# Two more gates computed by seven products, and a sigmoid moved, in a hybrid attention block

## The chip, the cores and the metric

The kernel runs on one core of one Trainium2 chip. The metric is device time in microseconds for one execution of the whole program; smaller is better. The time before is 1466.01 us, the median of three runs (1466.0 to 1467.67 us).

Five engines work side by side, each executing its own instructions in order: TensorE (PE, matrix products; its weight loads are listed as PEld), VectorE (DVE), ScalarE (ACT), GpSimd (POOL) and SyncE (SP), which issues the transfers between device memory and the core.

## The reference, cut to what matters

One layer over 1024 tokens of width 1024, in float32. A single input projection gives queries, keys and values for two branches of 8 heads each (64 columns a head) and two gates of 1024 columns each:

```
proj = x @ w_in                        # 1024 x 5120: 2 x (q, k, v of 512), 2 gates of 1024
yA = softmax attention over a band of 9 chunks of 64, with a bias by distance
yB = stick-breaking attention, strictly causal, in blocks of 128 queries
mix = sigmoid(gA + bA) * (yA @ w_proj_a) + sigmoid(gB + bB) * (yB @ w_proj_b)
x = LN(alpha * x + mix @ w_out)
x = LN(alpha * x + ffn(x))             # SwiGLU
```

In the kernel the gates are cut into 16 tiles of 128 channels by 1024 tokens, numbered 0 to 15. Tile 2c is channel group c of gate A, tile 2c + 1 the same group of gate B; "pair" c is both.

## The kernel before, in words

Every matrix product is made of three (high x high, high x low, low x high parts of its operands), so that it reaches float32 precision. One such matmul has a 128x128 weight and 512 columns.

The program is written as one list of steps in Python. A scheduler makes of it one instruction stream per engine when the kernel is built, and moves loads and other work ahead where their inputs allow it. Within an engine the stream is then fixed. Tiles live in pools with few buffers (`SLOTS`): 8 of kind `op` for loaded weights and reloaded data, 3 of kind `gt` for gates, 4 of kind `kp`. A load can be issued only when the buffer's last reader is done. All loads and stores go through SP in order.

- **Stage 1 (0 to 348 us), the input projection.** It runs over pairs of 128-column pieces of `w_in`. For a pair, `prep_left`, `prep_right` and `prep_last` (L128 to L157) load two weight tiles and build sums of them; `pair_steps` (L174) then does seven products instead of eight half products, each of 12 matmuls (`product`, L159 to L172), and DVE and ACT combine the results. Queries, keys, values and the first five gate pairs are made so: `work` (L221 to L229) lists them, `project` (L325) writes the results, and `out_g` (L363) stores a raw gate tile to device memory (`g_dr`). The bias of the gates, `bg`, is loaded after the third pair (L285).
- **Branch A (about 348 to 472 us), eight heads a0 to a7.** Each head has 12 value steps. ACT takes exponentials (L507), DVE maxima and reciprocals (L501, L511), POOL the scaling (L512), PE transposes (L570) and the products with the values (L583, L584); `pv` has one PSUM bank, which a copy on ACT or DVE (L591, L598) empties.
- **Branch B (about 472 to 675 us), eight heads b0 to b7.** The same value steps, with sigmoids (L539, L540), scans (L542) and a multiplication on POOL (L547).
- **Fillers.** Between the steps of the heads, matmuls of other work are put: a generator `fill_all` (L611) yields them one by one, and `FILL` (L39) says how many a head gets in branches A and B. They are, in order: the remaining gates, one at a time (`gate`, L414: 48 matmuls each, with a weight load, cast and subtraction by `load_w`, L397), and then the projection of branch A's output. For that, `reload_y` (L651) loads a tile of the attention's output, casts it on ACT (L656) and subtracts on POOL (L657); `reload_gate` (L659) loads a gate tile and takes its sigmoid on ACT; 24 matmuls per channel group (L630) and a multiplication on DVE (L633) follow. What is not done when the last head ends runs behind it.
- **Behind branch B (675 to 722 us)** the same is done for branch B's output (L747 to L764), with `reload_gate` for gate B. Then come the output projection, the layer norms and the FFN, in the same way as before and after the change.

The first branch's order is set by `vsteps` (L706 to L733): at each step a goal rises by `FILL[branch] / 12`, and fillers are emitted until their number reaches it:

```
goal += FILL[hd["br"]] / nhead
fill_until(0.5 * (last + goal))
...
fill_until(goal)
```

Of the kernel before, what the change touches and what calls it, by code (L numbers as in the profile page):

```python
# [13 lines left out]
AF = mybir.ActivationFunctionType  # L14
# [21 lines left out]
LAG = 2  # L36
LEAD = ((6, 7, 9, 9, 10, 10, 11, 11, 12, 12, 13, 13), (7, 8, 9, 9, 10, 10, 11, 11, 12, 12, 13, 14))

FILL = (18.0, 42.0)  # L39

# [5 lines left out]
def hybrid_trunk_kernel(ctx: ExitStack, tc, x, xt, w_in, b_gate, rel_bias, w_proj,  # L48
# [6 lines left out]
    nc = tc.nc  # L55
# [12 lines left out]
    def cycle(tags, name, dtype=F32):  # L68

        turn_of[tags] = turn_of.get(tags, -1) + 1  # L70
        return slot(tags[turn_of[tags] % len(tags)], name, dtype)
# [3 lines left out]
    def bank(tag, name):  # L75
        return ps.tile([P, HW], F32, tag=tag, name=name, bufs=BANKS[tag])
# [13 lines left out]
    bg = cst.tile([P, 16], F32, name="bg")  # L90
# [17 lines left out]
    def split(dst_h, dst_l, src):  # L108
        nc.scalar.copy(dst_h, src)  # L109
        nc.vector.tensor_tensor(dst_l, src, dst_h.bitcast(F32), ALU.subtract)  # L110
# [63 lines left out]
    def pair_steps(nm, W, ops, c, done, xtag="mm"):  # L174


        st = {}

        def begin(key, tag, p):
            st[key] = bank(tag, f"{key}{nm}")  # L180
            product(st[key], W, ops, p, True)

        def add(dst, src):
            nc.vector.tensor_tensor(dst, src, dst, ALU.add)  # L184

        def p1():
            begin("sx", xtag, 1)
            nc.scalar.copy(c("11"), st["sx"])

        def p2():  # L190
            begin("sy", "sc", 2)
            add(c("11"), st["sy"])
            done("11", None)

        def p6():
            product(st["sx"], W, ops, 6, False)
            nc.scalar.copy(c("12"), st["sx"])

        def p5():
            begin("sz", "sc", 5)  # L200
            nc.scalar.copy(c("22"), st["sz"])

        def p7():
            product(st["sx"], W, ops, 7, False)
            add(c("22"), st["sx"])
            done("22", None)

        def p3():
            product(st["sz"], W, ops, 3, False)
            add(c("12"), st["sz"])  # L210
            done("12", None)

        def p4():
            product(st["sx"], W, ops, 4, False)
            done("21", st["sx"])

        return [p1, p2, p6, p5, p7, p3, p4]
# [7 lines left out]
            if i % 2:  # L225
                work.append(("v", br * 4 + i - 1, br * 12 + 8 + i - 1, br * 12 + 8 + i))

    N_GATE = 5
    work += [("g", j, 24 + j, 32 + j) for j in range(N_GATE)]  # L229
    Wa = [dict() for _ in work]  # L230

# [3 lines left out]
    def right(i):  # L235
        prep_right(Wa[i], f"p{i}", w_in[work[i][3]], "op")
        prep_last(Wa[i], f"p{i}", "kp")
# [47 lines left out]
    def small_inputs():  # L285

        rel_sb = cycle(QKV, "rel_sb")[0:8, 0:896]
        rel_in = cycle(QKV, "rel_in")[0:8, 0:N_REL]
        dma(rel_in, rel_bias)
        nc.vector.tensor_copy(rel_sb[:, 383:896], rel_in[:, ::-1])  # L290
        nc.vector.tensor_copy(rel_sb[:, 0:383], rel_in[:, 512:513].to_broadcast([8, 383]))
        dma(rel_dr, rel_sb)
        dma(bg, b_gate)

    def store_hl(d, hi, lo):
        for h in range(2):
            rows = slice(h * DH, (h + 1) * DH)
            dma(d[h * P:h * P + DH], hi[rows].bitcast(F32))
            dma(d[h * P + DH:(h + 1) * P], lo[rows])
# [25 lines left out]
    def project(i):  # L325
        kind, pair = work[i][:2]
        tl = {}

        def tile_of(side):
            if side not in tl:  # L330
                tl[side] = cycle(QKV, f"c{side}_{i}")
            return tl[side]

        def c(name):
            return tile_of(name[1])[:, (LO, HI)[int(name[0]) - 1]]

        def out_qk(side):
            scale = (-0.125 if pair < 4 else 0.125) if side == "1" else 1.0
            t = tl[side]
            h = cycle(QKV, f"hi{side}_{i}", F32R)  # L340
            nc.scalar.activation(h, t, AF.Copy, scale=scale)
            nc.vector.scalar_tensor_tensor(t, t, scale, h.bitcast(F32), ALU.mult, ALU.subtract)
            d = (q_dr, k_dr)[side == "2"]
            store_hl(d[pair], h, t)

        def out_v(side):
            pr = pair + int(side) - 1
            vs = [cycle(QKV, f"v{pr}_{h}", F32R).rearrange("p (t c) -> p t c", t=8)
                  for h in range(2)]
            for hf in range(2):  # L350
                tp = bank("tr", f"vtp{pr}_{hf}")
                for j in range(4):
                    o = hf * HW + j * P
                    tr(tp[:, j * P:(j + 1) * P], tl[side][:, o:o + P], ident)
                t3 = tp.rearrange("p (t c) -> p t c", t=4)
                ts_ = slice(4 * hf, 4 * hf + 4)
                for h in range(2):
                    split(vs[h][:, ts_, 0:DH], vs[h][:, ts_, DH:P],
                          t3[:, :, h * DH:(h + 1) * DH])
            for h in range(2):  # L360
                dma(v_dr[2 * pr + h].rearrange("p (t c) -> p t c", t=8), vs[h].bitcast(F32))

        def out_g(side):  # L363
            dma(g_dr[2 * pair + int(side) - 1], tl[side])

        out = dict(qk=out_qk, v=out_v, g=out_g)[kind]

        def done(name, acc):
            if name == "21":
                nc.scalar.copy(c("21"), acc)  # L370
                out("1")
            elif name == "12":
                out("2")

        return pair_steps(f"p{i}", Wa[i], ops_x, c, done)
# [35 lines left out]
    def load_gate(i, lo_eng):  # L411
        return load_w(w_in[24 + (i % 2) * 8 + i // 2], f"g{i}", of("op"), of("op"), lo_eng)

    def gate(i, w):  # L414
        gt = slot("gt", f"gate{i}")
        for hf, cs in enumerate((LO, HI)):
            acc = bank("mm", f"gps{i}_{hf}")
            for k in range(KT):
# [13 lines left out]
              lambda i: right(i + 1), lambda i: small_inputs() if i == 2 else None)  # L432
    first_gate = 2 * N_GATE
    first_w = load_gate(first_gate, nc.vector)
# [176 lines left out]
    def fill_all():  # L611
        w = first_w
        for i in range(first_gate, 16):
            nxt = load_gate(i + 1, nc.gpsimd) if i < 15 else load_proj(0, 0, "op", nc.gpsimd)
            yield from gate(i, w)
            w = nxt
        for i in range(4):
            reload_y(i, nc.gpsimd)
        for cc in range(4):
            nxt = load_proj(0, cc + 1, "op", nc.gpsimd) if cc < 3 else None  # L620
            for j in range(2):
                c = 2 * cc + j
                t = slot("gt", f"gA{c}")
                reload_gate(t, c, 0)
                for hf, cs in enumerate((LO, HI)):
                    acc = bank("mm", f"yAps{c}_{hf}")
                    for k in range(4):
                        ks = slice(j * HW + k * P, j * HW + (k + 1) * P)
                        for n, (lw, rx) in enumerate(((w[0], yh), (w[0], yl), (w[1], yh))):
                            mm(acc, lw[:, ks], rx[k][:, cs], start=(k == n == 0),  # L630
                               stop=(k == 3 and n == 2))
                            yield 1.0
                    nc.vector.tensor_tensor(t[:, cs], acc, t[:, cs], ALU.mult)  # L633
                if c < KEEP:
                    dma(m_dr[c], t)
                else:
                    kept[c] = t
            if cc < 3:
                reload_y(4 + cc, nc.gpsimd)
            w = nxt  # L640
# [18 lines left out]
    def reload_gate(t, c, br):  # L659
        dma(t, g_dr[2 * c + br])  # L660
        col = br * 8 + c
        nc.scalar.activation(t, t, AF.Sigmoid, bias=bg[:, col:col + 1])

    fill = fill_all()
    state = dict(t=0.0, done=False)
# [1 line left out]
    def fill_until(t):  # L667
        while state["t"] < t and not state["done"]:
            try:
                state["t"] += next(fill)  # L670
            except StopIteration:
                state["done"] = True
# [36 lines left out]
    for si, (hd, g, st, box) in enumerate(vsteps):  # L709
# [17 lines left out]
        last = goal  # L727
        goal += FILL[hd["br"]] / nhead
        fill_until(0.5 * (last + goal))
# [395 lines left out]
```

## Time and profile before

| | |
|---|---|
| median of three runs | 1466.01 us |
| the profiled execution | 1465.81 us |
| its span, first to last instruction | 1464.0 us |
| mean granted TensorE clock | 0.995 of full speed |
| PE busy | 1432.2 us |
| DVE, ACT, POOL busy | 1025.3, 679.4, 278.1 us |
| instructions on PE, DVE, ACT, POOL | 6740, 1637, 1179, 326 |

A row of the timeline gives the start, the duration, the engine, the line of the kernel, the operation, and output<-input by the names of the tiles; in brackets stands how long the engine was idle just before, and what it waited for. A row of the chain gives the start, the duration and the work that the end of the program depended on at that time. The page's slices cut the span in 40 parts and give the busy share of each in tenths. A row of a tile's view gives line, engine, operation and count, then the shortest, median and longest duration in nanoseconds.

### The profile page before, as it was taken

To read this page: it belongs to the slowest core of one execution; us is meant where nothing else is said; L and a number is where in the kernel's file an instruction comes from. 1 tells how busy PE (TensorE), PEld (TensorE's weight loads), DVE (VectorE), ACT (ScalarE), POOL (GpSimd) and SP (SyncE) were. 2 spreads that over 40 slices of the span, in tenths; PEclk is the share of its full clock that TensorE was granted. 3 is DMA by queue.
4 is the path that set the end of the run, shared out by engine and by line. 5 is a ranking of instruction groups with operands and counts; after the bars stand their busy time and mean duration, and the time that the engine had idled before them with its cause. 6 is when DMAs were issued, how large, how long until landed. Compare 5 with 4: busy or idle time off the path is not lost.

```text
span 1464.0 us, 19115 instructions
## 1 busy us (share of the span) xinstructions
PE 1432.2 (98%) x6740; PEld 1184.4 (81%) x6740; DVE 1025.3 (70%) x1637; ACT 679.4 (46%) x1179; POOL 278.1 (19%) x326
## 2 busy tenths in 40 slices
PE   8999999999999998999999999999999999999997
PEld 6788888887888787878888888888888888888886
DVE  8856655434776876887848966777776665978767
ACT  6444444335878878775413534444444433221201
POOL 0000000003555879760004100000000000100016
PEclk9999999999999999999999999999999999999999
DMA  6565545338666476856611123444444457887602
GB/s 216 158 188 173 157 145 177 124 99 249 188 196 206 131 217 184 238 179 247 232 43 72 50 95 130 158 154 148 152 151 145 152 195 247 301 308 235 213 15 101
DMA packets 83455, 247.72 MB, mean 169 GB/s; under 512 B 10512, under 2 KB 10512, under 8 KB 83360
## 3 DMA queue, kind: packets, MB, share of 16 engines
q1 hardware_dynamic: 83360, 246.51, 51.5%
q8 instruction: 53, 0.87, 0.3%
q14 instruction: 42, 0.34, 0.1%
HBM read 162.03 MB, written 80.77 MB: 166 GB/s over the span
## 4 chain that ended last, share of the span: by engine, by line
PE 86%; DVE 5%; DMA 3%; ACT 3%; issue 2%; POOL 1%; SPq 0%; POOLq 0%; DVEq 0%; ACTq 0%
PE sxf L171 16%; PE sxp L171 12%; PE szf L171 8%; PE dx L1058 6%; PE szp L171 6%; PE syf L171 4%; PE gps L421 3%; PE dz L1058 3%; PE syp L171 3%; PE yAps L630 2%; PE ops L117 2%; PE ops L119 2%; PE ops L116 2%; PE fpswh_h L119 1%; PE fpswh_h L116 1%
## 5 line engine op out<-in xcount | busy, mean ns | idle before, releaser
L1014 POOL TENSOR_TENSOR wdyt<-wdyt 128x512 f32<-128x512 f32 x8 | 10.8, 1352 | 513.6 <-DMA wdgt<-in_w_ffn_out_dram 429.1
L547 POOL TENSOR_TENSOR w_b<-w_b,kp_b 128x511 f32<-128x511 f32 (+3 forms) x96 | 96.2, 1010 | 39.0 <-DVE kp_b L542 27.0
L542 DVE TENSOR_TENSOR_SCAN kp_b<-kp_b,ident_ps 128x512 f32<-128x512 f32 (+2 forms) x64 | 56.4, 883 | 24.8 <-ACT kp_b L539 24.3
L482 POOL MEMSET bias<- 64x64 f32 x8 | 1.2, 144 | 329.7 <-ACT bias L481 329.7
L778 POOL TENSOR_TENSOR mv<-mv,neghalf 128x1 f32<-128x1 f32 x16 | 23.8, 1489 | 210.3 <-DVE mv L777 210.3
L184 DVE TENSOR_TENSOR c<-sxp,c 128x512 f32<-128x512 f32 x16 | 11.1, 691 | 74.2 <-issue 41.1
L539 ACT ACTIVATE kp_b<-sc_b 128x512 f32<-128x512 f32 (+3 forms) x96 | 50.0, 521 | 24.9 <-PE sc_b L465 23.2
L110 DVE TENSOR_TENSOR pt_b<-tp_b,pt_b 128x512 fp32r<-128x512 f32 (+1 forms) x96 | 50.4, 543 | 13.8 <-ACT pt_b L109 13.5
L989 DVE TENSOR_TENSOR x<-dx,x 128x512 f32<-128x512 f32 x64 | 43.5, 686 | 17.0 <-PE dx L1058 16.9
L171 PE MATMUL szf<-x1S63h,wcf 128*128 128x512 f32 x168 | 55.1, 389 | 0.0
L109 ACT CAST pt_b<-tp_b 128x512 fp32r<-128x512 f32 (+1 forms) x96 | 48.2, 515 | 7.7 <-PE tp_b L570 6.1
L110 DVE TENSOR_TENSOR sl<-h,sl 128x512 fp32r<-128x512 f32 x56 | 38.4, 685 | 18.8 <-ACT sl L109 18.8
L512 POOL TENSOR_SCALAR w_a<-w_a,st_a 128x640 f32<-128x640 f32 (+2 forms) x64 | 42.6, 670 | 45.1 <-DVE st_a L511 33.5
L109 ACT CAST sl<-h 128x512 fp32r<-128x512 f32 x56 | 34.7, 619 | 34.5 <-PE syf L171 17.1
L110 DVE TENSOR_TENSOR pt_a<-tp_a,pt_a 128x512 fp32r<-128x512 f32 (+1 forms) x96 | 45.8, 486 | 6.8 <-ACT pt_a L109 5.5
L540 ACT ACTIVATE w_b<-sc_b 128x511 f32<-128x511 f32 (+3 forms) x96 | 50.2, 523 | 0.0
L570 PE MATMUL tp_b<-ident,w_b 128*128 128x128 f32 x288 | 48.7, 279 | 1.5 <-DVE pt_b L110 1.1
L116 PE MATMUL ops<-wh_o,mh 128*128 128x512 f32 x128 | 50.2, 392 | 0.0
L119 PE MATMUL ops<-wh_o,ml 128*128 128x512 f32 x128 | 50.0, 391 | 0.0
L117 PE MATMUL ops<-wl_o,mh 128*128 128x512 f32 x128 | 49.9, 390 | 0.0
L109 ACT CAST pt_a<-tp_a 128x512 fp32r<-128x512 f32 (+1 forms) x96 | 39.7, 426 | 19.2 <-PE tp_a L570 17.8
L507 ACT ACTIVATE w_a<-w_a,st_a 128x640 f32<-128x640 f32 (+2 forms) x64 | 44.7, 698 | 6.4 <-DVE st_a L501 5.9
(1883 smaller groups left out, 4811.4 us busy)
## 6 DMA issues: line engine op xcount, KB each, us to landing
s_dr<-sl SPq DMA_DIRECT2D x112, 256.0 KB, 2.1
sd<-s_dr SPq DMA_DIRECT2D x56, 512.0 KB, 4.5
wLf<-in_w_ffn_in_dram SPq DMA_DIRECT2D x22, 512.0 KB, 4.3
wRf<-in_w_ffn_in_dram SPq DMA_DIRECT2D x22, 512.0 KB, 3.6
wLp<-in_w_in_dram SPq DMA_DIRECT2D x17, 512.0 KB, 5.4
wRp<-in_w_in_dram SPq DMA_DIRECT2D x17, 512.0 KB, 4.2
v_dr<-v SPq DMA_DIRECT2D x16, 512.0 KB, 4.6
qs<-q_dr SPq DMA_DIRECT2D x16, 512.0 KB, 5.3
```

Of the source, the lines that this page charges most:

```text
L109: nc.scalar.copy(dst_h, src)
L110: nc.vector.tensor_tensor(dst_l, src, dst_h.bitcast(F32), ALU.subtract)
L116: mm(acc, lh, rh, start=(i == 0), stop=False)
L117: mm(acc, lh, rl, start=False, stop=False)
L119: mm(acc, ll, rh, start=False, stop=(i == n))
L171: mm(acc, lw[:, ks], rx, start=(first and kt == i == 0), stop=(kt == 3 and i == 2), skip_group_check=not first)
L539: nc.scalar.activation(kp[:, c0:e], sc[:, 0:n], AF.Sigmoid, scale=-1.0)
L540: nc.scalar.activation(be[:, m0:e], sc[:, m0 - c0:n], AF.Sigmoid)
L542: nc.vector.tensor_tensor_scan(kp[:, 0:e], kp[:, 0:e], ident_ps()[:, 0:e], 0.0, ALU.mult, ALU.add)
L547: nc.gpsimd.tensor_tensor(be[:, m0:e], be[:, m0:e], kp[:, m0 - 1:e - 1], ALU.mult)
L570: tr(tp[:, (qb - lo_q) * P:(qb - lo_q + 1) * P], wt[qb - q0][:, (kb - qb) * P:(kb - qb + 1) * P], ident)
L1058: mm(acc, a, b, start=(first and i == n == 0), stop=(i == n - 1 == 1), skip_group_check=not first)
```

## The change

The number of gate pairs that stage 1 computes by seven products rises from five to six: gates 10 and 11 leave the fillers, so that 12 of 16 gates are made in stage 1 and four (12 to 15) as fillers. For the 12, the sigmoid with its bias is taken in `out_g`, in place, before the store; `reload_gate` then takes it only for channel groups 6 and 7. `FILL` goes from 18 and 42 to 8 and 40 matmuls a head. The number of fillers falls from 480 (288 for gates, 192 for the projection) to 384 (192 and 192), and 8 x 8 + 8 x 40 = 384.

```
-FILL = (18.0, 42.0)
+FILL = (8.0, 40.0)
...
-    N_GATE = 5
+    N_GATE = 6
     work += [("g", j, 24 + j, 32 + j) for j in range(N_GATE)]
...
         def out_g(side):
+            col = (int(side) - 1) * 8 + pair
+            nc.scalar.activation(tl[side], tl[side], AF.Sigmoid, bias=bg[:, col:col + 1])
             dma(g_dr[2 * pair + int(side) - 1], tl[side])
...
     def reload_gate(t, c, br):
         dma(t, g_dr[2 * c + br])
         col = br * 8 + c
-        nc.scalar.activation(t, t, AF.Sigmoid, bias=bg[:, col:col + 1])
+        if c >= N_GATE:
+            nc.scalar.activation(t, t, AF.Sigmoid, bias=bg[:, col:col + 1])
```

From `out_g` on, the lines of the changed kernel have numbers higher by two (L507 before is L509 after), and by three behind `reload_gate`.

## The prediction

> **What bounds the kernel now.** I read the totals and the slices of the page first, then windows by stage, then PE's waits and the chain of work around the longest of them, and last ACT's timeline at the borders of the stages.
>
> ```profile
> PE 1432.2 (98%) x6740; PEld 1184.4 (81%) x6740; DVE 1025.3 (70%) x1637; ACT 679.4 (46%) x1179; POOL 278.1 (19%) x326
> PE   8999999999999998999999999999999999999997
> PE 86%; DVE 5%; DMA 3%; ACT 3%; issue 2%; POOL 1%; SPq 0%; POOLq 0%; DVEq 0%; ACTq 0%
> ```
>
> TensorE is the bound: busy 98% of the span, and 86% of the chain that ended last. A change pays through fewer or cheaper matmuls, or through the little idle time that PE has. The windows show where that is (columns: window, its length, then busy us and count for PE, PEld, DVE, ACT, POOL; granted clock; DMA share; GB/s).
>
> ```profile
> 271.66:290.70 19.04, 19.04 (x85) 15.77 (x84) 8.85 (x11) 6.03 (x9) 0.00 (x0) 1.00 0.33 111
> 348.00:472.00 124.00, 119.69 (x724) 102.41 (x724) 93.44 (x344) 98.10 (x244) 67.37 (x92) 1.00 0.70 196
> 472.00:675.00 203.00, 193.53 (x1050) 160.59 (x1049) 154.83 (x223) 160.36 (x351) 145.76 (x185) 0.97 0.63 190
> ```
>
> The first row is one whole gate pair of stage 1, from its first product to that of the next pair: PE has no gap, the other engines work less than half the time. Branch A (second row) has 4.31 us of PE idle time, branch B (third) 9.47 us, and there the clock is 0.97.
>
> **The change, part by part.**
>
> *Stage 1: one pair more, +19.04 us.* Pair 5 (gates 10 and 11) takes seven products of 12 matmuls, 84 in all; by the first row above that is 19.04 us, 0.2267 us a matmul. Its DVE work (8.85) and ACT work (6.03) lie beside PE. Its two weight loads replace the two that the gates had as fillers, and its two stores replace theirs.
>
> *The two gates leave the fillers, -21.77 us ideally.* They were 2 x 48 = 96 matmuls of the same 128x512 shape: 96 x 0.2267 = 21.77. So the saving in matmuls alone is 12 x 0.2267 = 2.72 us; the rest of the forecast is about waits. In the built instruction order of the two kernels, branch A (with what runs ahead of its first head) has 158 fillers before and 75 after; branch B has 322 and 309. That is 83 x 0.2267 = 18.82 in A and 13 x 0.2267 = 2.95 in B. The 83 are spread unevenly: ahead of the first head 14 become 21; head a0 8 becomes 5; a1 to a6, with 18 each, become 2, 2, 4, 8, 8, 8; a7 28 becomes 17. A's ACT and POOL also lose the work of the gates (casts, copies, subtractions); the bound below is a row of a head that had little of it.
>
> *What A loses by having fewer fillers, +3.5 us (0 to +8.2).* Fillers are what PE does while a head waits for its softmax.
>
> ```profile
> 357.01:373.06 16.05, 14.32 (x90) 12.13 (x88) 12.61 (x48) 11.94 (x34) 5.79 (x10) 1.00 0.77 176
> 373.06:389.63 16.57, 16.26 (x100) 13.99 (x99) 12.82 (x49) 14.15 (x38) 9.99 (x16) 1.00 0.63 175
> 439.34:455.90 16.56, 16.11 (x103) 14.10 (x102) 12.35 (x44) 12.80 (x32) 9.80 (x12) 1.00 0.70 212
> 360.09 0.53 PE L465 MATMUL sc_a<-kl,qs 128*128 128x320 f32 x2 [0.98 <-DMA kl<-k_dr]
> 372.43 0.41 PE L464 MATMUL sc_a<-kh,qs 128*128 128x320 f32 x1 [0.52 <-DVE st_a L501]
> ```
>
> The three windows are heads a0 (8 fillers), a1 and a5 (18 each). With 18 fillers PE is idle 0.31 and 0.45 us a head; with 8 it is idle 1.73, of which 0.98 is the wait for a load of keys (fourth row), so 0.75 by itself, 0.52 of that in one wait for DVE's row maximum (last row). The slope is (0.75 - 0.31) / 10 = 0.044 us a filler. So a1 and a2 would be idle 1.01 and a3 0.93, where a head of 18 has 0.31: +2.0 together; a4 to a6 0.44 more each: +1.3; a0 +0.13. That is +3.5. Heads of two fillers would then need 16.57 - 16 x 0.2267 + 0.70 = 13.6 us, for which DVE has 12.6 and ACT under 12.8 us of work: tight, so the lower end (PE stays as busy as now, 0) is not the likely one. The upper end is that no head gets shorter than a0 without its load, 16.05 - 0.98 = 15.07. Then a1 to a6 save 6 x 1.50 = 9.0 and not the 76 x 0.2267 = 17.2 that their fillers held: +8.2. I take 3.5, the slope of the neighbouring rows.
>
> *Start of A, +0.5 us (0 to +2.4).* The sigmoid of gate 11 now follows the last DVE sum of pair 5, and ACT must then change its table to the exponential.
>
> ```profile
> 348.51 1.05 ACT L404 CAST wh_g<-wr_g 128x1024 fp32r<-128x1024 f32 x1
> 349.67 0.83 ACT L507 ACTIVATE w_a<-w_a,st_a 128x640 f32<-128x640 f32 x1
> L662 ACT ACTIVATE gA<-gA,bg x8: 1151/1154/1463, 565.1 to 645.4; 128x1024 f32<-128x1024 f32 x8
> 469.18 1.28 ACT L539 ACT_TABLE_LOAD   x1
> 470.47 0.60 ACT L539 ACTIVATE kp_b<-sc_b 128x512 f32<-128x512 f32 x1
> 471.09 1.28 ACT L507 ACT_TABLE_LOAD   x1
> 472.90 1.28 ACT L540 ACT_TABLE_LOAD   x1
> ```
>
> In the built order sigmoid and table load stand between this cast and the first exponential: 1.15 + 1.28 = 2.43 us later. On SP the loads of head a1's keys and queries are queued behind the gate stores, which now wait for the sigmoids. Seven more fillers, 1.59 us, lie ahead of the first head. 2.43 - 1.59 = 0.84 would remain if nothing else covers it, and 2.43 if PE runs the fillers too soon; I take 0.5. The row at 470.47 begins 0.01 us after the load ends, so a table costs 1.28 on ACT here. The Trainium skill ("ScalarE: Activation LUTs", section "What ACT_TABLE_LOAD costs") says a switch is 1.28 us and a drain of 1.38 behind it, 2.66 in all; the trace shows no such drain, and by the page this term would be up to 1.4 higher.
>
> *The other sigmoids and tables, 0.* The ten others in stage 1 take 1.15 us each, 2.3 a pair, where ACT has 13 of 19 us free; one of them brings a table load (1.28). They leave branch B and the stage behind it. At the border of A and B (rows above) three table loads become one. That is 2.56 us less of ACT, but PE has fillers there (42 a head), so I count nothing, down to -1.3.
>
> *Stall 1 in branch B, -5.0 us (-6.5 to 0).* The longest wait of the stage comes from the reload of the attention's output for branch A's projection (chain of work first, then the timeline):
>
> ```profile
> 565.80 2.38 POOL yl L657
> 568.19 6.98 DMA yraw<-y_dr
> 576.52 0.60 ACT yv_b L598
> 568.04 1.46 ACT L662 ACTIVATE gA<-gA,bg 128x1024 f32<-128x1024 f32 x1
> 575.20 1.04 ACT L656 CAST yh<-yraw 128x1024 fp32r<-128x1024 f32 x1 [3.91 <-DMA yraw<-y_dr]
> 577.16 0.80 PE L583 MATMUL pv_b<-pt_b,v 128*128 128x512 f32 x1 [3.50 <-ACT yv_b L598]
> 560.00:580.00 20.00, 16.09 (x78) 12.53 (x77) 12.59 (x18) 15.42 (x31) 20.00 (x22) 0.91 0.84 224
> 577.16:584.20 7.04, 7.04 (x24) 6.13 (x25) 4.40 (x8) 5.47 (x11) 6.96 (x6) 0.58 0.18 58
> ```
>
> The load of the fifth y tile waits for a buffer until POOL's subtraction ends, takes 6.98 us to land, and ACT, which executes in order, stands 3.91 us at its cast (L656) with the copy that PE needs (L598) queued behind. PE loses 3.50, and then 7.04 x (1 - 0.58) = 2.96 to the clock: 6.5 in all. In the built order of the changed kernel the first four reloads and their subtractions stand earlier against attention, since the gates end 13 fillers sooner; the fifth load is issued behind the store of gate 15, and 19 ACT instructions stand between that gate's last copy and the cast. At 15.42 / 31 = 0.50 us each that is 9.5 us, against 7 for the load and some 2 for four SP issues ahead of it. So the load lands about in time. POOL has no slack there (20.00 of 20.00), and the next weight, two ACT instructions later, lands behind it: I leave 1.5 us of wait. Without the earlier order 6.5 would stay. What is late next is that weight's cast.
>
> *The two smaller stalls, -0.5 and +0.5 us.*
>
> ```profile
> 601.60 1.15 ACT L662 ACTIVATE gA<-gA,bg 128x1024 f32<-128x1024 f32 x1 [1.39 <-DMA gA<-g_dr]
> 603.65 0.50 PE L583 MATMUL pv_b<-pt_b,v 128*128 128x512 f32 x1 [1.04 <-ACT yt L598]
> 648.24 1.09 ACT L656 CAST yh<-yraw 128x1024 fp32r<-128x1024 f32 x1
> 650.20 1.05 ACT L404 CAST wh_y<-wr_y 128x1024 fp32r<-128x1024 f32 x1 [0.49 <-DMA wr_y<-in_w_proj_dram]
> 653.87 0.50 PE L583 MATMUL pv_b<-pt_b,v 128*128 128x512 f32 x1 [1.94 <-DVE yt L591]
> 653.87:658.37 4.50, 4.50 (x19) 4.00 (x19) 4.29 (x8) 2.48 (x6) 2.79 (x3) 0.62 0.30 84
> ```
>
> At 601.60 ACT waits for a gate's load before a sigmoid that the change takes away; half of PE's 1.04 us, as the multiplication (L633) still needs the load: -0.5 (-1.04 to 0). At 653.87 PE waits 1.94 us and loses 4.50 x 0.38 = 1.71 to the clock. The last reload (L656) now stands five ACT instructions earlier and may wait longer for its data, while the sigmoid at 645 stays: +0.5 (-3.65, the stall gone, to +3.65, one such stall more).
>
> On the clock, the row at 577.16 stands behind 3.50 us of idle PE and the row at 653.87 behind 1.94, both at about 0.6; behind 1.04 us at 603.65 no drop follows. So a wait of about 2 us counts nearly double. The Trainium skill ("TensorE: Matmul & The Clock Gate", "What's actually happening") ties the slow state to an idle window of about 3.4 us. The first stall agrees, the second (1.94 us) does not. By the page what I leave of stall 1 would not touch the clock; by the trace, at 2 us, it would add up to 1.7.
>
> *The sum.* 19.04 - 18.82 + 3.5 + 0.5 - 2.95 - 5.0 - 0.5 + 0.5 = -3.7 us on the profiled execution's 1465.81 (span 1464.0 and 1.81 around it): 1462.1. That execution is 0.20 below the median 1466.01, so 1462.3.
>
> **Rivals.**
>
> *Slower: A's heads keep nearly the length they have, 0.25.* If loads of keys, or the chain from scores over DVE's maximum to the exponential, set a head's time once the fillers are gone, the heads a1 to a6 don't shrink. For: a0 with 8 fillers took 16.05 against 16.57, saving 0.52 of the 2.27 us that its ten fillers less should give. Against: 0.98 of it is one load. At 15.07 a head the change would give -3.7 + 4.7 = +1.0; each 0.1 more adds 0.6, so it is slower than now by 2.9 from 15.4 on. Halfway between the two readings (15.56) it is +3.9: 1470.
>
> *No change: stall 1 stays, 0.28.* For: the fifth load now stands on SP behind a store that waits for gate 15's copy, and POOL is full. With 3.50 us and its clock left the sum is -3.7 + 5.0 = +1.3: 1467.3. The A term at 15.07 gives the same class.
>
> *Faster than I say, 0.12.* A stays bound by PE (0 for 3.5) and stall 1 goes whole: -3.7 - 3.5 - 1.5 = -8.7: 1457.3.
>
> **How the numbers follow.** My own case has 0.35, its range 1459 to 1463.1. With the last rival, faster has 0.47; no change (within 2.9 us, 0.2%, about what can be told here) 0.28; slower 0.25. The range goes from the good case to just under the slower rival: 1457.5 to 1469.5.
>
> **What would show it.** Stage 1 must end 19 us later with PE full. The windows of a1 to a3 should be 13.3 to 14 us; at 15 or more the A term failed. PE's wait for yv_b (L598) in branch B should be below 2 us and the clock near 1.00; a wait of 3 or more, or a new one for a projection weight, breaks the largest gain. The border of A and B should show one table load. The forecast falls if branch A is not at least 14 us shorter, or if branch B's clock is still 0.97.

## The result, and the profile after

The changed kernel takes 1457.59 us (median of six runs, 1456.72 to 1459.25); the kernel before took 1466.01. The ratio is 0.9944 with a 95% interval of 0.9931 to 0.9956: 8.4 us faster, where 3.7 were forecast. The time lies 0.09 us inside the low end of the range of 1457.5 to 1469.5, next to the rival "faster than I say" (1457.3).

The page of the changed kernel, totals:

```profile
PE 1426.8 (98%) x6728; PEld 1178.7 (81%) x6728; DVE 1027.9 (71%) x1648; ACT 679.2 (47%) x1181; POOL 274.2 (19%) x324
```

The 12 matmuls fewer are there. PE's busy time fell by 5.4 us and not by the 2.72 of those matmuls. The rest is mostly clock, since a busy PE at a lowered clock counts as busy: in branch B (rows below) busy time fell by 7.00 us, where 13 fillers fewer hold 2.95. To see where the span went, I cut both traces at the same four events: the last matmul of stage 1, the first product with the values in head b0, the first matmul of branch B's projection, and the first of the output projection. The columns are as in the prediction's windows. Before:

```profile
347.60:490.79 143.19, 137.52 (x824) 116.32 (x822) 108.44 (x368) 116.17 (x287) 83.80 (x117) 1.00 0.68 192
490.79:675.42 184.63, 176.52 (x954) 147.44 (x955) 140.04 (x200) 142.71 (x308) 129.60 (x164) 0.97 0.63 193
720.20:1464.00 743.80, 734.87 (x3269) 606.93 (x3267) 534.99 (x747) 250.23 (x349) 61.01 (x35) 1.00 0.44 154
```

After:

```profile
366.93:491.86 124.93, 119.37 (x741) 100.93 (x739) 105.31 (x368) 110.17 (x283) 79.00 (x114) 1.00 0.71 205
491.86:665.57 173.71, 169.52 (x941) 141.77 (x942) 137.22 (x200) 133.48 (x299) 130.54 (x164) 1.00 0.65 206
710.21:1455.90 745.69, 735.63 (x3269) 606.70 (x3267) 534.79 (x747) 250.04 (x349) 60.89 (x35) 1.00 0.43 154
```

| part | before | after | difference | forecast |
|---|---|---|---|---|
| stage 1 | 347.60 | 366.93 | +19.33 | +19.04 |
| branch A | 143.19 | 124.93 | -18.26 | -14.8 |
| branch B | 184.63 | 173.71 | -10.92 | -7.95 |
| projection of branch B | 44.78 | 44.64 | -0.14 | 0 |
| output projection to the end | 743.80 | 745.69 | +1.89 | 0 |
| span | 1464.0 | 1455.9 | -8.1 | -3.7 |

Two things stand out: the clock in branch B is back at 1.00, and the last part, which the change does not touch, takes 1.9 us longer. The stall that cost most lay in head b3. The timeline and the window of that head, after (the load of the fifth y tile, its cast, and the copy behind it):

```profile
563.16 0.53 SPq L655 DMA_DIRECT2D yraw<-y_dr  x1
570.57 1.09 ACT L658 CAST yh<-yraw 128x1024 fp32r<-128x1024 f32 x1
571.89 0.64 ACT L600 COPY yv_b<-pv_b 128x512 f32<-128x512 f32 x1
558.24:580.46 22.22, 22.22 (x125) 18.79 (x124) 18.51 (x27) 17.51 (x41) 22.22 (x25) 1.00 0.81 251
```

The load is issued 7.4 us ahead of its cast; before, it was 7.0 us, and ACT stood idle for 3.91 of them. Now the cast waits for nothing, and PE has no idle time in the head: 22.22 us, against 30.02 for b3 before. The table load at the start of branch A and the last pair of the FFN's first part, after:

```profile
368.80 1.15 ACT L365 ACTIVATE c<-c,bg 128x1024 f32<-128x1024 f32 x1
369.97 1.28 ACT L509 ACT_TABLE_LOAD   x1
371.26 0.83 ACT L509 ACTIVATE w_a<-w_a,st_a 128x640 f32<-128x640 f32 x1
1222.89 0.62 ACT L109 CAST wdc<-wdyt 128x512 fp32r<-128x512 f32 x1 [2.44 <-DMA wdyt<-in_w_ffn_out_dram]
1223.42 1.05 ACT L109 CAST wdl2h<-wdgt 128x1024 fp32r<-128x1024 f32 x1
1226.38 0.72 PE L171 MATMUL sxf<-x1A,wbf21h 128*128 128x512 f32 x2 [1.12 <-DVE gt L184]
```

The sigmoid and the table load stand ahead of the first exponential as forecast, and the next instruction begins 0.01 us behind the load. The border of A and B has one table load, at 473.5 us, in place of three; the moved sigmoids are not the reason, as the kernel without them (below) has one as well and the kernel with them alone has three. In the FFN ScalarE waits 2.44 us for a load and PE then 1.12 us. Before, the same two casts stood the other way round:

```profile
1230.52 1.05 ACT L109 CAST wdl2h<-wdgt 128x1024 fp32r<-128x1024 f32 x1
1232.57 0.62 ACT L109 CAST wdc<-wdyt 128x512 fp32r<-128x512 f32 x1 [1.00 <-PE sxf L171]
1235.08 0.62 PE L171 MATMUL sxf<-x1A,wbf21h 128*128 128x512 f32 x2
```

The scheduler orders the whole program, and an edit to the first 670 us changed the order of two casts at 1220 us.

### The profile page after: what moved, and what is told of

The parts are those of the page before. It is cut to its first block, busy times and chain, and to the rows that moved or that the text cites. A ratio compares the mean times of both kernels' runs of the same rounds, so it can differ in the third digit from the quotient of the medians.

```text
span 1455.9 us, 19099 instructions
## 1 busy us (share of the span) xinstructions
PE 1426.8 (98%) x6728; PEld 1178.7 (81%) x6728; DVE 1027.9 (71%) x1648; ACT 679.2 (47%) x1181; POOL 274.2 (19%) x324
## 4 chain that ended last, share of the span: by engine, by line
PE 86%; DVE 6%; ACT 2%; DMA 2%; issue 2%; POOL 1%; SPq 1%; POOLq 0%; DVEq 0%; ACTq 0%
PE sxf L171 15%; PE sxp L171 12%; PE szf L171 7%; PE szp L171 6%; PE dx L1061 6%; PE syf L171 4%; PE dz L1061 3%; PE syp L171 3%; PE gps L423 2%; PE yAps L632 2%; PE ops L117 2%; PE ops L119 2%; PE ops L116 2%; PE fpswh_h L116 2%; PE fpswh_h L119 1%
## 5 line engine op out<-in xcount | busy, mean ns | idle before, releaser
L895 ACT ACTIVATE h<-sxf 128x512 f32<-128x512 f32 x21 | 12.5, 597 | 72.8 <-PE sxf L171 72.8
L509 ACT ACTIVATE w_a<-w_a,st_a 128x640 f32<-128x640 f32 (+2 forms) x64 | 44.8, 702 | 3.1 <-DVE st_a L503 2.7
```

## The experiments

All ratios are to the kernel before, run on the same chip beside them. I first asked which part of the change gives the gain. My theory was the place of the reloads in branch B; the rival was the sigmoids.

**Gates and fillers without the sigmoids.**

```
 N_GATE = 6;  FILL = (8.0, 40.0)
-            nc.scalar.activation(tl[side], tl[side], AF.Sigmoid, ...)   # out_g
-        if c >= N_GATE:                                                # reload_gate
+        always the sigmoid
```

> The twelve gates by seven products and the new filler numbers, but every sigmoid stays where it was (in the reloads). Theory (place): the gain is 2.7 us of matmuls and the removal of the long wait in branch B, which goes because the fifth reload is issued earlier against attention; the sigmoids play no part. Then the time is within 2 us of the changed kernel: 1456 to 1460, with no wait of PE over 2 us for the copy of yv_b. Rival (sigmoids): the wait goes because ACT has fewer sigmoids in branch B. Then a wait of 3 us or more with a low clock stays, and the time is 1462 to 1465.

1462.34 us, ratio 0.9975 (0.9963 to 0.9987). The wait for yv_b is gone and the clock is full, as the theory says, but the time is at the rival's: 4.7 us above the changed kernel. The rows of PE that speak, for head a1's keys and at b4, then branch A and branch B by the cuts above:

```profile
380.24 0.38 PE L464 MATMUL sc_a<-kh,qs 128*128 128x320 f32 x1 [2.48 <-DMA kh<-k_dr]
602.20 0.38 PE L464 MATMUL sc_b<-kh,qs 128*128 128x256 f32 x1 [0.72 <-ACT w_b L540]
603.38 0.63 PE L570 MATMUL tp_b<-ident,w_b 128*128 128x128 f32 x4 [0.68 <-DVE pt_b L110]
366.38:494.27 127.89, 119.71 (x740) 100.52 (x738) 105.19 (x368) 107.64 (x280) 79.15 (x115) 1.00 0.73 198
494.27:669.68 175.41, 170.17 (x944) 141.97 (x944) 137.65 (x200) 140.49 (x307) 130.41 (x164) 1.00 0.63 204
```

Both theories had a part: the long wait is gone without the sigmoids, and the sigmoids cost something else. In this execution more of it lies in branch A (127.89 us against 124.93 in the changed kernel) than in branch B (175.41 against 173.71).

**The sigmoids alone.** Five pairs, fillers 18 and 42, the sigmoid in `out_g` and not in the reloads.

> The sigmoid moved into the first stage for the ten gates that are already made there, and nothing else (five pairs, fillers 18 and 42). Place: 1465 to 1467, the wait of about 3.5 us for yv_b and the clock near 0.6 behind it stay. Sigmoids: 1459 to 1462, the long wait goes.

1462.31 us, ratio 0.9972 (0.9960 to 0.9985): the move alone gives 4.1 us, and neither expectation holds whole. The long wait stays, but its clock costs less:

```profile
576.10 0.79 PE L585 MATMUL pv_b<-pt_b,v 128*128 128x512 f32 x1 [3.25 <-ACT yv_b L600]
576.10:580.00 3.90, 3.90 (x13) 3.29 (x14) 2.15 (x4) 3.32 (x7) 3.90 (x5) 0.63 0.22 67
```

3.25 us of wait and 3.90 x 0.37 = 1.4 us of clock, where the kernel before lost 3.50 and 3.0. Between the two profiled executions branch B is 2.4 us shorter, of which b3, with its clock, has 1.6; branch A is 0.5 shorter.

**The place alone.**

```
-FILL = (18.0, 42.0)
+FILL = (19.75, 40.25)
```

> The kernel before with fillers of 19.75 and 40.25 a head in place of 18 and 42: in the built order branch A has 173 fillers in place of 158, and the first matmul of the projection of branch A comes 8 to 9 matmuls earlier in head b3. No work is saved or moved between stages. Place: the long wait shrinks or goes, 1459 to 1463. Sigmoids: unchanged, 1465 to 1467.

1460.23 us, ratio 0.9957 (0.9945 to 0.9970): 6.2 us for two numbers, with no work saved. No wait for yv_b is left. Its head b3:

```profile
560.89:583.69 22.80, 22.50 (x125) 18.69 (x124) 18.82 (x27) 21.15 (x45) 22.80 (x26) 1.00 0.75 241
```

30.02 us became 22.80. So most of the stall's removal has nothing to do with the gates.

**The changed kernel with the place put back.**

```
-FILL = (8.0, 40.0)
+FILL = (6.25, 41.75)
```

> The changed kernel with fillers of 6.25 and 41.75: the projection of branch A starts at the ninth filler of head b3, as in the kernel before (tenth), and not at the fortieth of b2. Place: a wait of 3 us or more comes back near the fifth reload, with its clock: 1462 to 1465. Sigmoids: 1457 to 1459.

1462.32 us, ratio 0.9972 (0.9961 to 0.9982). The stall is back, in another shape: not a load but POOL. The timeline (POOL, ACT, PE) and the window behind it:

```profile
575.95 2.38 POOL L659 TENSOR_TENSOR yl<-yraw,yh 128x1024 fp32r<-128x1024 f32 x1
578.30 2.38 POOL L407 TENSOR_TENSOR wl_y<-wr_y,wh_y 128x1024 fp32r<-128x1024 f32 x1
580.69 1.28 POOL L549 TENSOR_TENSOR w_b<-w_b,kp_b 128x511 f32<-128x511 f32 x1
582.00 0.60 ACT L541 ACTIVATE kp_b<-sc_b 128x512 f32<-128x512 f32 x1 [3.32 <-POOL w_b L549]
586.56 1.09 PE L572 MATMUL tp_b<-ident,w_b 128*128 128x128 f32 x4 [1.72 <-DVE pt_b L110]
586.56:593.50 6.94, 6.94 (x25) 5.79 (x26) 3.73 (x5) 1.70 (x5) 5.10 (x8) 0.59 0.47 146
```

Two subtractions, one of a reload and one of the next weight, stand ahead of the attention's multiplication on POOL; ACT waits 3.32 us, PE 1.72, and then 6.94 x 0.41 = 2.8 us go to the clock. The time is the one expected for the place; the wait of PE is shorter than the 3 us expected with it.

**Which sigmoids.** Two halves of the move, in the changed kernel: only those of gate A in the first stage, and only those of gate B.

```
+            if side == "1":            # the other kernel: "2"
                 nc.scalar.activation(tl[side], tl[side], AF.Sigmoid, ...)
-        if c >= N_GATE:
+        if c >= N_GATE or br == 1:     # the other kernel: br == 0
```

> The changed kernel, but only the sigmoids of gate A are taken in the first stage; those of gate B stay in their reloads behind branch B. With all sigmoids in the reloads the time was 1462.3, with all in the first stage 1457.6. Branch theory: what the move gives is ACT time in branch B, where the reloads of gate A stand among the attention's casts and copies. Then nearly all of the 4.7 us is here: 1457 to 1459, and PE's waits in heads b4 to b6 are those of the changed kernel. Rival (start of A): the gain comes from the sigmoids and the table load that stand ahead of branch A's first exponential, which make the scheduler put more fillers there and issue the loads of the second head in another order. This kernel has 17 fillers ahead of the first head, against 16 with no sigmoid moved and 21 with all, so the rival says 1461 to 1463.

> The other half: only the sigmoids of gate B in the first stage, those of gate A stay in branch B's reloads. Branch theory: 1461 to 1463, with waits for exponentials and transposes near heads b4 to b6 as in the kernel without any sigmoid moved. Start of A: 15 fillers ahead of the first head, like none moved, so 1461 to 1463 as well; a time of 1457 to 1459 would speak against both, for then what matters is merely that the schedule is another.

Gate A: 1459.70 us, ratio 0.9965 (0.9951 to 0.9979). Gate B: 1461.81, ratio 0.9973 (0.9962 to 0.9984). By the ratios, since these two ran on another chip, that is 5.1 and 4.0 us below the kernel before, against 3.7 with no sigmoid moved and 8.2 with all. The intervals of either half and of none overlap, so the times do not tell which half gives more. Branch A and branch B by the same cuts, first with gate A's sigmoids moved, then with gate B's, and last branch B of the kernel with another order of two casts (below):

```profile
367.11:491.89 124.78, 119.93 (x742) 101.21 (x740) 104.90 (x368) 109.58 (x282) 78.50 (x112) 1.00 0.71 204
491.89:667.69 175.80, 170.36 (x942) 143.18 (x942) 137.55 (x200) 135.52 (x301) 130.34 (x164) 0.99 0.66 204
```

```profile
366.04:491.67 125.63, 119.90 (x741) 101.20 (x739) 105.25 (x368) 108.94 (x282) 78.87 (x114) 1.00 0.74 203
491.67:668.18 176.51, 170.93 (x942) 143.31 (x942) 137.82 (x200) 139.21 (x305) 130.54 (x164) 0.99 0.66 203
```

```profile
491.62:667.49 175.87, 169.35 (x941) 141.84 (x942) 137.27 (x200) 133.59 (x299) 130.41 (x164) 1.00 0.64 203
```

With gate A's half moved, branch A takes 124.78 us, as in the changed kernel (124.93) and not as without any (127.89); branch B takes 175.80, no less than without any (175.41). So this execution speaks against the branch theory: what gate A's half gives lies in branch A, where the rival looked. The last row shows how far branch B can be read. That kernel has the changed kernel's order of instructions in branch B on every engine, and yet its execution takes 175.87 us there, where the changed kernel's took 173.71 (head b4 25.15 and 24.11, b6 27.26 and 25.74). A difference of some 2 us in branch B between two single executions, and what b4 or b6 add to it, therefore shows nothing by itself.

**Seven pairs.** `N_GATE = 7`, fillers 4 and 32, then 6 and 30.

> One more pair: seven pairs by seven products, fillers 4 and 32 (288 in all). Matmuls: 12 fewer again, 2.7 us. In the built order the last pair of the FFN's first part has its two casts in the order of the kernel before, so the new wait of 1.1 us on PE there (sxf for gt) should be gone: another 1.4. If the first branch stays bound by PE with 2 fillers a head, and no long wait appears in branch B: 1452.5 to 1455. If heads a3 to a6, now at 2 fillers each, take over 13 us, or branch B with 32 fillers a head is held by GpSimd: 1456 to 1460.

> Seven pairs with fillers 6 and 30, the projection starting at the twelfth filler of head b1 and not at its twenty-sixth as with 4 and 32 (1463.7 us). With 4 and 32 the reloads fell into b1 and b2, which took 22.0 and 24.4 us against 20.7 to 21.1 for b3 to b5. If it is the place alone: 1455 to 1460. If too few fillers are left in branch B for what its other engines need: 1461 to 1466.

1463.71 us, ratio 0.9985 (0.9975 to 0.9995), and 1462.04, ratio 0.9975 (0.9966 to 0.9984): 4.5 to 6.1 us slower than six pairs with 8 and 40, though 12 matmuls fewer. The first time lies above both ranges expected, the second in that for too few fillers. A third kernel of seven pairs, with fillers 8 and 28, gave no time. Branch A is not the main reason: it is shorter than with six pairs in both kernels. Its head a2 with 2 fillers, in the kernel with 4 and 32, and then head b1 in that with 6 and 30:

```profile
425.94:438.26 12.32, 11.82 (x79) 10.26 (x78) 10.95 (x42) 11.07 (x31) 7.94 (x14) 1.00 0.77 227
```

```profile
527.50:553.23 25.73, 22.06 (x115) 18.21 (x116) 18.56 (x26) 19.26 (x44) 25.34 (x28) 0.93 0.59 175
```

A's heads are short and PE is nearly full. Head b1, where the first reloads fall, takes 25.73 us, and POOL is busy for 25.34 of them; PE runs dry and the clock drops. With so few fillers in a head, I read, PE's work no longer covers the reload's work on POOL; a kernel with the reloads spread over more heads, which would test it, was not run. The place is a rival: the projection starts here at the twelfth filler of its head, near the places that stall with fewer pairs (below). What the two kernels also show: their cast order in the FFN is that of the kernel before, and from the output projection on they take 743.8 and 744.0 us.

**The order of two casts.**

```
             c = W["c"] = take(f"wdc{f}")
+            if f == 2:
+                nc.scalar.copy(c[:, 0:1], W["12"][0][:, 0:1])
```

> The changed kernel with one tiny copy more on ScalarE (128x1), which forces the cast of wdl2h ahead of that of wdc in the last pair of the FFN's first part, the order that the kernel before has. Theory: from the first matmul of the output projection to the end the kernel before takes 743.8 us and the changed one 745.7, because there ScalarE stands 2.4 us at wdc's cast for a load, and PE then waits 1.1 us. Every kernel so far with that cast order has an end of 745.0 to 746.1, every one with the other order 743.8 to 744.2. So the end should take 744 and the whole 1455.5 to 1456.5, with no wait of sxf for gt. Rival: the end is longer for another reason, and stays at 745 to 746: 1457 to 1458.

1455.95 us, ratio 0.9936 (0.9920 to 0.9952). The intervals of this ratio and of the changed kernel's overlap, so the whole time alone would not settle it; the part does:

```profile
712.03:1455.50 743.47, 734.58 (x3269) 606.97 (x3267) 534.93 (x747) 250.51 (x350) 61.06 (x35) 1.00 0.42 155
```

743.47 us in place of 745.69, and no wait of sxf for gt is left.

**Other places, with that order.** Fillers 9 and 39, and 12 and 36.

> The same with fillers 9 and 39: branch A has 81 fillers instead of 75, and the projection of branch A starts six matmuls earlier, at the thirty-fourth of head b2. If the place of the reloads against attention is what costs or saves the long wait, and only the late side is bad, the time is that of the kernel with 8 and 40 and the same order of casts, within 1.5 us: 1454.5 to 1457.5. If 8 and 40 is a lucky place between bad ones, 1458 or more.

> The same with fillers 12 and 36: 104 in branch A, the projection starts at the seventeenth filler of head b2. Only the late side is bad: 1454.5 to 1458. Lucky place, or branch B's heads too empty at 36 a head: 1459 to 1464.

9 and 39 give 1454.72 us (1454.0 to 1455.53), ratio 0.9928 (0.9914 to 0.9942): the lowest median here, 2.9 us below the changed one, though the intervals of the two ratios overlap. 12 and 36 give 1457.28, ratio 0.9948 (0.9933 to 0.9963); on the same chip each of its runs is slower than each with 9 and 39. That is inside the expectation, but not for its reason: a stall is back, now in head b2 (the heads b1, b2 and b3).

```profile
517.27:538.34 21.07, 21.07 (x122) 17.92 (x120) 16.88 (x24) 17.49 (x41) 15.65 (x22) 1.00 0.76 247
538.34:565.98 27.64, 24.72 (x121) 20.35 (x121) 19.08 (x27) 21.76 (x48) 27.48 (x29) 0.88 0.68 222
565.98:587.00 21.02, 21.02 (x122) 18.12 (x120) 17.97 (x27) 15.97 (x38) 17.32 (x24) 1.00 0.47 151
```

b2 takes 27.64 us with POOL busy for 27.48 of them, and the clock at 0.88. So "only the late side is bad" falls: an earlier place can be bad too. Heads too empty at 36 fillers do not explain it alone, as b1 and b3 have as many and PE has no idle time in them.

Early and late may not be what matters. Over all kernels here, the projection starts at the ninth to the seventeenth filler of a head in the five that have such a stall with a low clock in that head or the next (the kernel before, the sigmoids alone, the place put back, 12 and 36, and seven pairs with 6 and 30). It starts at the first, the thirty-fourth or the fortieth in the eight that have none there, and at the twenty-sixth in the one between (seven pairs with 4 and 32: no drop of the clock, but a head of 24.39 us). That the place within a head is the cause was not tested.

**The sigmoids at the best place.** Fillers 9 and 39 and the forced order, every sigmoid back in the reloads.

> Fillers 9 and 39 with the forced order of casts (1454.7 us), but every sigmoid back in the reloads. With 8 and 40 the move of the sigmoids was worth 4.7 us on top of the gates, with five pairs 4.1 alone. If that is what ScalarE's time in branch B and the start of branch A cost in general, this takes 1458 to 1461. If it was an accident of two schedules, 1454 to 1457.

1458.76 us, ratio 0.9951 (0.9933 to 0.9968): 4.0 us above 1454.72 (3.4 by the ratios, whose intervals overlap; but each run here is slower than each of the other kernel's). The move was worth 4.1, 4.7 and 4.0 us in three surroundings, so it is no accident of one schedule. Between these last two profiled executions, branch B differs by 2.7 us, branch A by 1.0 and the projection behind branch B by 0.9.

## Why the prediction was right or wrong

*Right in direction, half the size.* The forecast was -3.7 us, the result -8.4. The table above gives the terms. That the time still lies in the range, by 0.09 us, is luck. What came is the rival with 0.12, "faster than I say": branch A stayed bound by PE and stall 1 went whole. That its number fits too (1457.3) is luck again, as the 1.9 us lost at the end of the program, which no term held, met some 1.5 us gained in branch B beyond that rival's terms.

*Stage 1: right.* +19.33 for +19.04.

*Branch A: the penalty was too large by 3.5 us.* I took +3.5 for heads with few fillers and +0.5 for the start; what came is 18.82 - 18.26 = 0.56 for both. The failed step is the slope of 0.044 us a filler, drawn from head a0. The window of 373.06 to 389.63, which I called head a1, is not a head either: it is 0.66 us longer than a1, though its idle time is the same. Cut from first product to first product, the heads before were, and after are (a1 first, then a2):

```profile
373.06:388.97 15.91, 15.60 (x98) 13.48 (x97) 12.16 (x47) 13.49 (x37) 9.61 (x15) 1.00 0.62 168
388.97:404.97 16.00, 15.62 (x98) 13.56 (x97) 12.26 (x46) 12.47 (x33) 9.23 (x12) 1.00 0.80 246
```

```profile
392.98:405.56 12.58, 12.27 (x82) 10.63 (x81) 11.48 (x45) 11.39 (x34) 7.18 (x12) 1.00 0.77 218
405.56:417.87 12.31, 11.81 (x79) 10.26 (x78) 10.94 (x42) 11.06 (x31) 7.86 (x13) 1.00 0.76 224
```

With 2 fillers PE is idle 0.31 and 0.50 us, not the forecast 1.01; before, with 18, it was 0.31 and 0.38. The 1.73 us of head a0 belong to the start of the branch, not to its few fillers. DVE's and ACT's work falls with the gates' (from 12.2 to about 11.2 and from 13 to about 11.2 us), so they hold nobody up. That also ends the rival "slower": A's heads with two fillers went to 12.3 to 12.6 us, far below the 15.4 from which it would have decided.

*Start of A: the sign was wrong.* The sigmoid and the table load are there, and the lead to the first product grew from 9.41 to 11.01 us, about the 1.59 of the seven more fillers. But I expected a loss of 0.5, and the loads of a1's keys queued behind the stores; what came is that PE no longer waits for these keys. That wait was 0.98 us before. In the kernels that leave gate A's sigmoids in the reloads it is 0.98, 2.02 (the place alone), 2.48 (gates and fillers without the sigmoids), 1.43 (gate B's half) and 1.76 (9 and 39 without the move); in the nine that move them it is gone.

*Stall 1: right, and whole.* I forecast -5.0 with 1.5 us left. Nothing was left, and the load issued earlier against attention, the reason I gave, is what the kernels with the place alone and with the place put back show. In head b3 it is -7.80, two fillers (0.45) among it. What I had not seen is that POOL's queue can make the same stall at a later and at an earlier place.

*The sigmoids: the step that failed most.* Twelve are moved, so beside gate 11's there are eleven others and not ten. I counted them at nothing but half a wait (-0.5), and a small loss at the start of A. Alone they gave 4.1 us, and 4.7 on top of the gates. I had looked in branch B, for one wait behind a sigmoid. A part of the gain lies at the start of branch A. Without the move, the lead and head a0 take 26.68 us and hold 20 fillers; in the changed kernel they take 26.05 us and hold 26. With 9 and 39 it is 26.00 us and 20 fillers without the move, 26.05 us and 26 fillers with it. Six fillers are 6 x 0.2267 = 1.36 us, so the start of A is worth some 2.0 us in the first case and 1.3 in the second. Whether the key loads' order or the six fillers ahead of them end the wait, no run separates. The rest would be in branch B, where the sigmoids stand on ACT's queue among the attention's copies and casts (1.7, 2.4 and 2.7 us in the three pairs of executions); that is argued and not shown, as one order of instructions alone differed by 2.2 us there.

*The smaller stalls: open.* At 603 the wait of 1.04 went, as forecast, and waits of 0.86 and 0.67 for the transposes came in head b4. The stall at 653 went too, with its clock; a wait of 1.37 took its place, where I had +0.5. What b4 and b6 gained or lost by it cannot be said, for the reason above.

*The clock: the rule was wrong.* I wrote that a wait of about 2 us counts nearly double. The waits of 2.48 and 2.02 us for keys were followed by no drop, and neither was one of 1.96 us in head b6 with 9 and 39; the last section has what the traces show instead.

*The end of the program: not in the forecast.* I took the part behind branch B to run in the same way before and after. Its order changed, and cost 1.9 us; forcing the order back gave 2.2 in that part.

*The sum.* Branch A 3.5 and branch B 3.0 more than forecast, less 1.9 at the end and 0.3 in stage 1, with 0.1 behind branch B: the 4.4 us between -3.7 and the -8.1 of the profiled spans. Of the 3.0, up to 2.2 may be the scatter of branch B.

## What to carry to other kernels

Where a filler stream carries loads, casts and subtractions with it, its place against the main stream can be worth more than the matmuls that are saved: two numbers gave 6.2 us here, 12 matmuls some 2.7 by their rate in stage 1, so after any change of filler numbers the place has to be looked at again on both sides. Small work on an engine with room can be worth moving: sigmoids of 1.15 us, on an ACT that was busy less than half the time, gave about 4 us three times, a part of it at the start of branch A, where a wait for keys went with them. When a scheduler orders the whole program, compare the part behind the change as well, and cut heads at the same event before measuring their length. Two executions of one order show how much of a difference between single profiles is scatter.

## What the runs showed of the hardware

Almost the same wait of PE cost very different amounts of clock: 3.50 us in the kernel before was followed by 7.04 us at 0.58, 3.25 us in the kernel with the sigmoids alone by 3.90 us at 0.63. The granted clock in the traces shows the difference. It goes to one half, for 6.83 us in the first case and for 3.41 us in the second; windows that reach beyond the drop show 0.58 to 0.63. The two drops of the kernel before, the first of the kernel with the sigmoids alone, and a wait without any drop (9 and 39, head b6) with the window around it:

```profile
576.31:583.12 6.81, 5.96 (x19) 5.19 (x20) 4.10 (x7) 5.66 (x12) 6.81 (x7) 0.50 0.18 58
654.80:658.20 3.40, 3.40 (x14) 2.98 (x13) 3.27 (x7) 2.15 (x4) 2.62 (x3) 0.50 0.24 53
```

```profile
575.60:579.00 3.40, 2.90 (x8) 2.42 (x9) 1.74 (x3) 2.83 (x6) 3.40 (x6) 0.50 0.36 120
```

```profile
642.76 0.41 PE L572 MATMUL tp_b<-ident,w_b 128*128 128x128 f32 x2 [1.96 <-DVE pt_b L110]
640.80:650.00 9.20, 7.24 (x43) 5.99 (x44) 9.20 (x14) 7.79 (x18) 5.51 (x6) 1.00 0.48 172
```

Between 30 and 1440 us, the 14 kernels show 11 drops. All last 3.41 or 6.83 us, and where one execution has two, they lie a whole multiple of 3.41 us apart. The length of a wait alone does not decide: 1.72 and 1.94 us were followed by a drop, 2.48, 2.02 and 1.96 were not. Cut into stretches of 3.41 us at the times of the drops, the traces show PE busy for 0.20 to 0.59 of the stretch ahead of a drop. Every stretch at full clock with a share below 0.47 was followed by a drop, none with one above 0.59, and between the two both occur. So the waits and gaps of one such stretch seem to count together, and it matters where in it a wait falls. The Trainium skill ("TensorE: Matmul & The Clock Gate", "What's actually happening") says that the activity window runs freely, and it puts the drop behind at least one idle window of about 3.4 us. The spacing of the drops, 3.41 us or whole multiples of it, agrees with both the free running and the length; but no drop here has a wholly idle stretch ahead of it, and PE was busy for up to 0.59 of one.
